# Waiting for the last six stores on GpSimd outside the hand-synchronised section, against registers, in place of SyncE inside it

## Chip, cores, metric

One core of one Trainium2 chip. The metric is the device time of one execution in microseconds (us), lower is better. The program runs on one core only; all runs were at a granted clock of 1.0.

## The reference

```python
x = x.astype(float32)                      # B, S, D = 8, 4096, 2112
pooled = x.reshape(B, S // 4, 4, D).mean(axis=2)
out = x - repeat(pooled, 4, axis=1)        # each group of 4 rows minus its mean
```

The input and the output have 276.8 MB each.

## The kernel before

Four neighbouring rows of x lie on one partition (4 x 2112 numbers), 128 groups make a tile, and there are n = 64 tiles of 4224 KB. Six buffers ("slots") take turns. SyncE issues all loads, VectorE adds the four rows and subtracts the mean in place, ScalarE issues all stores. Everything is synchronised by hand, inside a section in which the framework adds no waits of its own. Each store adds 16 to the semaphore of its slot when it has landed.

```python
    laps, rest = divmod(n, SLOTS)                       # 10, 4
    with tc.tile_critical():                            # the hand-synchronised section
        for k in range(n):                              # SyncE: loads
            b, lap = k % SLOTS, k // SLOTS
            load = nc.sync.dma_start(out=slots[b][:], in_=xg[k * P:(k + 1) * P])
            if lap:
                load._wait_ge(store_sems[b], 16 * lap)  # the slot's last store has landed
            load.then_inc(load_sems[b], 16)
        with nc.vector.Fori(0, laps):                   # VectorE: a loop of 6 tiles a lap
            for b in range(SLOTS):
                reduce_tile(b, b % 2)
        for b in range(rest):                           # and 4 tiles written out
            reduce_tile(b, b % 2)
        for k in range(n):                              # ScalarE: stores
            store = nc.scalar.dma_start(...)            # cut
            store._wait_ge(done_sem, k + 1)
            store.then_inc(store_sems[b], 16)
        for k in range(n - SLOTS, n):                   # SyncE: the last six stores have landed
            nc.sync.wait_ge(store_sems[k % SLOTS], 16 * (k // SLOTS + 1))
```

## Time and profile before

| | before |
|---|---|
| median of 6 runs | 1285.78 us (1285.68 to 1285.93) |
| span of the profiled run | 1283.86 us |
| DMA | 553.66 MB at 431 GB/s, busy in all 40 slices |
| VectorE | 1026.5 us, 80% |
| last store issued, landed | 1268.6, 1282.3 us |
| from there to the end | 1.56 us |

The time is that of the span and about 1.8 us around it.

### The profile page before, as it was taken

Reading aid. Unit: us, or ns where it says so; the run is one execution under the profiler, and the core shown is the slowest. Engines: PE = TensorE matmul, PEld = TensorE weight load, DVE = VectorE, ACT = ScalarE, POOL = GpSimd, SP = SyncE. Lnnn points to the kernel's source line nnn. Section 1 sums busy time; section 2 is a strip of 40 time slices with the busy share of each in tenths; the row PEclk is TensorE's granted clock in tenths of the full one; section 3 lists DMA queues with packets and bytes.
Section 4 is the critical chain, followed back from the end, with each engine's and each line's share of the span. In section 5 each row is a group of like instructions: output and inputs, shape, how many; then the busy total and the mean of one; then the engine's idle time right before and its main releaser. Section 6 shows DMA issues by size and latency. Waiting matters only on the chain. (4 is left out here: it accounts for less than half of the span.)

```text
span 1283.9 us, 588 instructions
## 1 busy us (share of the span) xinstructions
DVE 1026.5 (80%) x256; POOL 0.2 (0%) x4
## 2 busy tenths in 40 slices
DVE  5998788787787877878778787787887877878775
POOL 0000000000000000000000000000000000000000
DMA  9999999999999999999999999999999999999999
GB/s 404 421 437 432 429 438 431 434 433 438 431 429 438 435 433 430 438 431 430 437 437 431 430 438 431 435 432 438 431 429 438 435 433 430 438 431 432 435 437 389
DMA packets 18433, 553.66 MB, mean 431 GB/s; under 512 B 2048, under 2 KB 2048, under 8 KB 2048
## 3 DMA queue, kind: packets, MB, share of 16 engines
q1 hardware_dynamic: 9216, 276.83, 50.1%
q10 hardware_dynamic: 9216, 276.83, 49.9%
q14 instruction: 1, 0.01, 0.0%
HBM read 276.82 MB, written 276.82 MB: 431 GB/s over the span
## 5 line engine op out<-in xcount | busy, mean ns | idle before, releaser
L67 DVE SCALAR_TENSOR_TENSOR slot<-s_sb,slot 128x8448 f32<-128x8448 f32 x32 | 286.7, 8959 | 4.7 <-DVEq L66 0.2
L67 DVE SCALAR_TENSOR_TENSOR slot<-s_ps,slot 128x8448 f32<-128x8448 f32 x32 | 286.6, 8957 | 4.7
L59 DVE TENSOR_TENSOR s_sb<-slot 128x2112 f32<-128x2112 f32 x32 | 75.5, 2358 | 120.5 <-DVEq L58 120.5
L59 DVE TENSOR_TENSOR s_ps<-slot 128x2112 f32<-128x2112 f32 x32 | 75.7, 2367 | 107.8 <-DVEq L58 107.8
L62 DVE TENSOR_TENSOR s_ps<-s_ps,slot 128x2112 f32<-128x2112 f32 x64 | 151.4, 2366 | 2.2
L62 DVE TENSOR_TENSOR s_sb<-s_sb,slot 128x2112 f32<-128x2112 f32 x64 | 150.9, 2358 | 2.2
L114 POOL MEMSET const-bfloat16-1.0<- 128x1 bf16 x1 | 0.1, 102 | 0.0
L114 POOL MEMSET const-uint8-127<- 128x1 uint8 x1 | 0.1, 102 | 0.0
L114 POOL MEMSET const-float32-0.0<- 128x1 f32 x1 | 0.1, 99 | 0.2 <-issue 0.2
L114 POOL MEMSET const-float32-1.0<- 128x1 f32 x1 | 0.1, 99 | 0.0
## 6 DMA issues: line engine op xcount, KB each, us to landing
slot<-in_x_dram SPq DMA_DIRECT2D x64, 4224.0 KB, 59.7
out_dram<-slot ACTq DMA_DIRECT2D x64, 4224.0 KB, 43.6
```

The lines of the kernel that those rows point to most:

```text
L59: add = nc.vector.tensor_add(out=s[:], in0=rows[:, 0, :], in1=rows[:, 1, :])
L62: add = nc.vector.tensor_add(out=s[:], in0=s[:], in1=rows[:, f, :])
L67: nc.vector.scalar_tensor_tensor(out=rows, in0=s[:, None, :].to_broadcast([P, STRIDE, D]), scalar=-1.0 / STRIDE, in1=rows, op0=mybir.AluOp ...
L114: nc = _bacc.Bacc("TRN2", target_bir_lowering=False, num_devices=1)
```

## The change

Its intent: SyncE has no work at the end, so its six waits keep the section open until the last store has landed, and the framework's own steps for leaving the section come after that (line 78 from 1282.4 us on in the trace of before). If an engine that has no part in the section waits instead, the section can be left early. The constants go into registers because the build doesn't take the same waits with constants there: the framework's model of the program reports a deadlock.

```diff
--- before.py
+++ after.py
@@ -95,8 +95,10 @@
             store._wait_ge(done_sem, k + 1)
             store.then_inc(store_sems[b], 16)
 
-        for k in range(n - SLOTS, n):
-            nc.sync.wait_ge(store_sems[k % SLOTS], 16 * (k // SLOTS + 1))
+
+    for k in range(n - SLOTS, n):
+        total = nc.gpsimd.to_reg(16 * (k // SLOTS + 1))
+        tc.keep_in_program_order(nc.gpsimd.wait_ge(store_sems[k % SLOTS], total))
 
 
 # ---- launch: one core; inputs and outputs as the reference has them ----
```

Where the waits end up in the built program is worth knowing. They carry no dependence on the section, so the framework puts them *ahead* of it in the engine's program. For GpSimd, which has nothing else to do, that makes no difference: it stands in the first wait from 0.7 us on. The same lines with SyncE or ScalarE were found to deadlock, since the engine would wait for the stores before issuing its own loads or stores.

## The prediction

> **What bounds the kernel now.** I read the page from the top: first the busy time of the engines, then the DMA row of the 40 slices, then the queues and HBM traffic, because a kernel that only loads, subtracts a mean and stores is either bound by VectorE or by its transfers.
>
> ```profile
> DVE 1026.5 (80%) x256; POOL 0.2 (0%) x4
> DMA  9999999999999999999999999999999999999999
> q1 hardware_dynamic: 9216, 276.83, 50.1%
> q10 hardware_dynamic: 9216, 276.83, 49.9%
> HBM read 276.82 MB, written 276.82 MB: 431 GB/s over the span
> ```
>
> The first line says that VectorE, the only computing engine, has a fifth of the span free. The second has a 9 in every slice: the 16 DMA engines are never seen idle. The queue lines give each queue's packet time as a share of 16 engines' span: 50.1% + 49.9% = 100%, one queue for the loads and one for the stores. So the bound is the traffic: 553.66 MB, each byte of x read once and each byte of the result written once, at 431 GB/s over 1283.9 us. No engine's work can shorten this while the bytes and the rate stay.
>
> Next the waits of the issuing queues, to see whether any transfer starts late.
>
> ```profile
> SPq L81 <- DMA out_dram<-slot: 1168.9, 58, 50.6
> SPq L99 <- DMA out_dram<-slot: 89.5, 3, 69.6
> ```
>
> The columns are total us, times, longest. Line 81 is the load: SyncE waits for a store to give a slot back before each of the 58 loads after the first six, which is the sign of a full pipe and not of a late issuer. Line 99 is the one that the change deletes: the six waits at the end, 89.5 us of SyncE standing still, of which 69.6 us is one wait. That number looks like a prize and isn't one: SyncE has no load left to issue then. Whether the wait costs anything is decided by what comes after it, so I looked at the last stretch.
>
> ```profile
> 1239.59 8.96 DVE L67 SCALAR_TENSOR_TENSOR slot<-s_sb,slot 128x8448 f32<-128x8448 f32 x1
> 1248.58 20.35 ACTq L94 DMA_DIRECT2D out_dram<-slot  x2
> 1252.29 2.37 DVE L59 TENSOR_TENSOR s_ps<-slot 128x2112 f32<-128x2112 f32 x1 [3.74 <-DVEq L58]
> 1254.68 4.77 DVE L62 TENSOR_TENSOR s_ps<-s_ps,slot 128x2112 f32<-128x2112 f32 x2
> 1259.60 8.96 DVE L67 SCALAR_TENSOR_TENSOR slot<-s_ps,slot 128x8448 f32<-128x8448 f32 x1
> ```
>
> This timeline (start us, duration us) shows the last subtraction ending at 1259.60 + 8.96 = 1268.56; the last two stores are issued at 1248.58 and, 20.35 us later at the end of the merged row, by 1268.93. The last store takes 13.7 us from issue to landing, so it lands at 1282.3. The span ends at 1283.9. Only this last 1.5 us, after the last landing, is within the reach of the change.
>
> ```profile
> 1252.00:1262.00 10.00, 9.50 (x4) 0.00 (x0) 1.00 1.01 433
> 1262.00:1272.00 10.00, 6.55 (x1) 0.00 (x0) 1.00 1.00 433
> 1272.00:1282.00 10.00, 0.00 (x0) 0.00 (x0) 1.00 0.88 378
> 1282.00:1284.00 2.00, 0.00 (x0) 0.00 (x0) 1.00 0.00 0
> ```
>
> In these stretches (stretch, length, VectorE, GpSimd, clock, DMA share, GB/s) the DMA engines are full up to 1272 us, 88% full in the next ten (data stops near 1280.8), and empty in the last two.
>
> [...] data stops near 1280.8 and the last wait ends at 1282.3, 1.5 us. [...] The trace has steps of 0.04 to 0.16 us between instructions of the exit[...]
>
> **The change part by part.** The built programs of both kernels are equal on VectorE, ScalarE and TensorE. SyncE loses the six waits, all other instructions stay in place. GpSimd gains six constants put into registers and six waits. It has no work between its start-up and the final barrier, so it arrives at these at about 0.7 us and stands there.
>
> Removed: SyncE's waits. In the trace the last of them ends at 1282.32. Then come, all within the chain that sets the end, the steps by which the hand-synchronised section is left:
>
> ```profile
> L78 SPq EVENT_SEMAPHORE  x2: 17/22/28, 1282.5 to 1282.7; - x2
> L78 SPq COMPARE_BRANCH  x1: 33/33/33, 1282.4 to 1282.4; - x1
> L78 ACTq DRAIN  x1: 8/8/8, 1282.6 to 1282.6; - x1
> L78 DVEq DRAIN  x1: 17/17/17, 1282.6 to 1282.6; - x1
> L78 SPq DRAIN  x1: 7/7/7, 1282.6 to 1282.6; - x1
> L78 SPq NOP  x1: 17/17/17, 1282.8 to 1282.8; - x1
> ```
>
> (Durations ns, then first and last start.) SyncE signals that the section is over, the three engines drain and answer, SyncE collects, and only then reports to the final barrier, at 1282.92. That is 1282.92 - 1282.32 = 0.60 us in series. After the change none of it waits for stores: SyncE can signal after its last load, and ScalarE and VectorE follow once the last store is issued at 1268.93. The 0.60 us then runs at about 1269.5, hidden beside the last store, which lands 13 us later.
>
> Added: GpSimd wakes when the last store lands, drains, and takes the barrier's count, where the other four engines have long been. The gap between neighbouring GpSimd sequencer steps in the exit of before is 0.08 to 0.16 us. Five of the six waits are satisfied before the last landing (the stores land 10 us apart), so they cost nothing; the last needs about two steps, wait to drain and drain to barrier: 2 x 0.08 = 0.16 us, call it 0.15 to 0.20.
>
> Unchanged: from the barrier's count at 1282.96 to the end at 1283.86, 0.90 us: release, clearing of the semaphores, a second barrier.
>
> Sum: the count is taken at 1282.32 + 0.18 = 1282.50 in place of 1282.96, so the end moves by -0.46 us. The span becomes 1283.4 and the time 1285.78 - 0.46 = 1285.32, a gain of 0.04%.
>
> **Rivals.**
> First, *the register wait is slow to wake*[...]. For it: nothing in the trace of before shows such a wait, so I have no duration. Against it: GpSimd already sits the whole run in a barrier wait and answers in 0.08 us. If each wake took 0.5 us, the time would be 1285.8; if 1 us, 1286.3.
>
> Second, *all 89.5 us of SyncE's wait count*, and the freed engine gives them back. For it: it is SyncE's second largest wait. Against it: no load follows, and the DMA row is full until 1281. It would make 1196 us[...]. I give it no weight.
>
> Third, *a waiting GpSimd disturbs the stream*[...], delaying DMA issues. Issues take 0.34 us of every 20 us, so even doubled they hide behind queued transfers, as the six slots keep transfers ahead. It would leave the time at 1285.3; only a slowing of the data itself by 1% would make 1298, and nothing in the profile speaks for it.
>
> Fourth, *the exit shortens further*: SyncE's last drain comes 0.45 us after the first release while the other engines take 0.1 to 0.2, perhaps because it has just branched. If it is ready earlier, another 0.2 us goes: 1285.1.
>
> **Range and chances.** The three runs of before lie within 0.19 us of each other. Around 1285.32 I allow the exit 0.2 us more gain or 0.5 us less, and the run-to-run scatter 0.2 to 0.3 us: 1284.8 to 1286.0. A change of over 2% means 25.7 us, over sixteen times all that happens after the last landing, so the chance of same is 0.98, and what is left is split evenly.
>
> **What would show it right or wrong.** Right: the DMA row full, both queues near 50%, span 1283.3 to 1283.6; SyncE's waits with no line for the end of stores; the section's exit on SyncE, ScalarE and VectorE near 1269 us; a GpSimd wait ending near 1282.3, and GpSimd's barrier step under 0.3 us later. Wrong in the wake-up: more than 0.3 us between the last landing and GpSimd's next step. Wrong in the hiding: the section's exit still after 1282. Wrong altogether: DMA share below 9 in a slice before the last, or the last landing moved by more than 1 us, which would mean that the waiting engine matters to the transfers.

Its sum came to 1282.50 in place of 1282.96 us for the count, -0.46 us, and 1285.32 us in all. Against the second rival stands that no load follows and that the DMA row has a 9 in all 40 slices.

## The result and the profile after

| | before | after |
|---|---|---|
| median, 6 runs each | 1285.78 us (1285.68 to 1285.93) | 1285.16 us (1285.12 to 1285.55) |
| ratio | | 0.9996 (95%: 0.9983 to 1.0009) |
| again later, 9 and 5 runs (e5 below) | 1285.68 us | 1285.19 us (1284.99 to 1285.39) |

Ratios are the mean time of one kernel's runs over that of the other's of the same rounds, so not quite the ratio of the medians. The difference of 0.05% is within the interval. The prediction was 1285.3 in a range of 1284.8 to 1286.0. All that follows is about tenths of a microsecond. The interval of the ratio can't show such a difference, but the profiles give the time of each instruction, and the runs of one kernel mostly lie within a few tenths of each other. Where medians are compared below, those of before come from the same rounds.

The page after, engines, DMA row and queues:

```profile
DVE 1026.4 (80%) x256; POOL 0.2 (0%) x4
DMA  9999999999999999999999999999999999999999
q1 hardware_dynamic: 9216, 276.83, 50.1%
q10 hardware_dynamic: 9216, 276.83, 50.0%
```

The same bound as before: the DMA engines full in every slice, two queues of one half each. The waits of SyncE (total us, times, longest):

```profile
SPq L81 <- DMA out_dram<-slot: 1168.9, 58, 50.4
SPq L78 <- DVEq L78: 75.7, 1, 75.7
SPq L127 <- PEq L127: 14.4, 2, 13.9
```

The line for the end of the stores (89.5 us before) is gone. In its place SyncE waits 75.7 us for VectorE's drain in the leaving of the section, line 78, and then, at line 127, stands in the final barrier for the rest. The total of waiting hasn't shrunk, and needn't: a waiting SyncE costs nothing here, with the DMA engines full in all 40 slices before and after. What moved is *what comes after the wait*. The instructions of line 78 in the profile after (durations ns, then first and last start in us), to be held against those of before in the prediction:

```profile
L78 SPq NOP  x2: 13/13/13, 0.7 to 1269.1; - x2
L78 SPq EVENT_SEMAPHORE  x2: 17/37818/75619, 1192.8 to 1193.0; - x2
L78 SPq DRAIN  x1: 58/58/58, 1192.9 to 1192.9; - x1
L78 DVEq DRAIN  x1: 8970/8970/8970, 1259.6 to 1259.6; - x1
L78 ACTq DRAIN  x1: 153/153/153, 1268.9 to 1268.9; - x1
```

Before, they started at 1282.4 to 1282.8. Now SyncE's begin at 1193, and all, the other engines' too, have ended by 1269.2. (SyncE's long EVENT_SEMAPHORE is a wait for two semaphores: in the trace it starts at 1192.99, 0.07 us after SyncE's own drain has ended, and ends at 1268.61, 0.03 us after VectorE's.) The end of the profile after, line 127, from 1282 us on:

```profile
L127 POOLq DRAIN  x3: 34/41/82, 1282.9 to 1283.5; - x3
L127 POOLq COMPARE_BRANCH  x1: 33/33/33, 1282.8 to 1282.8; - x1
L127 SPq DRAIN  x1: 7/7/7, 1283.2 to 1283.2; - x1
```

GpSimd branches at 1282.8, drains, and takes the barrier's count. (The build packs waits into neighbouring instructions: the branch itself carries the last of the six waits and starts 25 ns after the last store's last increment, so I take its start as the wake-up.) Before, from 1282 us on (the line numbers of the framework's end are 2 lower there):

```profile
L125 POOLq EVENT_SEMAPHORE  x4: 17/17/17, 1283.0 to 1283.8; - x4
L125 SPq DRAIN  x3: 7/7/130, 1282.9 to 1283.5; - x3
```

Beside the missing exit, a second difference is to be seen: SyncE had a drain of 130 ns at 1283.5 before; after, its only drain in this stretch takes 7 ns and starts at 1283.2. And a third works against the change. The last store, from issue to landing, before and after:

```profile
DMA to landing us min/median/max: 13.7/13.7/13.7
```

```profile
DMA to landing us min/median/max: 14.2/14.2/14.2
```

It landed half a microsecond later in this profile. The chain after the last landing, instruction by instruction as the trace has it (us):

| step | before | after (first profile) | after (e5) |
|---|---|---|---|
| 15th of 16 increments of the last store's semaphore | 1282.076 | 1282.035 | 1281.998 |
| 16th increment: landed | 1282.303 | 1282.752 | 1282.385 |
| the waiting engine wakes | 1282.320 (SyncE) | 1282.777 (GpSimd) | 1282.409 (GpSimd) |
| GpSimd takes the first barrier's count | 1282.955 | 1283.010 | 1282.643 |
| GpSimd takes the second barrier's count | 1283.679 | 1283.528 | 1283.161 |
| end | 1283.861 | 1283.712 | 1283.344 |
| wake to first count | 0.635 | 0.233 | 0.234 |
| first count to end | 0.906 | 0.702 | 0.701 |

So in the first profile: -0.40 us up to the first barrier, -0.20 us in the second, +0.46 us from a landing that was late by one increment of sixteen: together -0.15, which is the difference of the spans (1283.86 and 1283.71). In e5 the landing is late by only 0.08 us and the span shorter by 0.52.

### The profile page after: what moved, and what is told of

Same layout as the page of the kernel before. It is cut to its first block, busy times and chain, and to the rows that moved or that the text cites. A ratio compares the mean times of both kernels' runs of the same rounds, so it can differ in the third digit from the quotient of the medians.

```text
span 1283.7 us, 591 instructions
## 1 busy us (share of the span) xinstructions
DVE 1026.4 (80%) x256; POOL 0.2 (0%) x4
## 5 line engine op out<-in xcount | busy, mean ns | idle before, releaser
L59 DVE TENSOR_TENSOR s_ps<-slot 128x2112 f32<-128x2112 f32 x32 | 75.7, 2366 | 108.2 <-DVEq L58 108.2
```

The costliest lines, as they stand in the source:

```text
L59: add = nc.vector.tensor_add(out=s[:], in0=rows[:, 0, :], in1=rows[:, 1, :])
```

## The experiments

My theory after the first profile: the place of the wait (outside the section) takes 0.40 us off the chain, something on SyncE gives another 0.20, and the late landing has nothing to do with the change. Rivals: the form of the wait (registers) or the engine is what counts; a register wait wakes late; the late landing is caused by the change.

| run | what | median us | before, same rounds | difference |
|---|---|---|---|---|
| e1 | SyncE inside, registers | 1285.92 | 1285.63 | +0.29 |
| e2 | GpSimd inside, constants | 1285.40 | 1285.63 | -0.23 |
| e3 | SyncE in a second section, constants | 1285.97 | 1285.63 | +0.34 |
| e4 | changed, waits in opposite order | 1285.52 | 1285.63 | -0.11 |
| e5 | changed again | 1285.19 | 1285.68 | -0.49 |
| e6 | TensorE in GpSimd's place | 1285.24 | 1285.68 | -0.44 |
| e7 | changed, 16 more VectorE instructions | 1285.29 | 1285.68 | -0.39 |
| e8 | changed, 6 met waits on SyncE | 1285.29 | 1285.68 | -0.39 |
| e9 | changed, 18 met waits on SyncE | 1285.22 | 1285.68 | -0.46 |
| e10 | changed, 8 VectorE instructions fewer | 1285.03 | 1285.68 | -0.65 |
| e11 | before, 8 VectorE instructions fewer | 1285.47 | 1285.68 | -0.21 |

Five runs of each kernel, nine of before in each of three groups (e1 to e4, e5 to e7, e8 to e11). All gave the correct result, and every ratio to before has an interval that holds 1.

**e1: the form of the wait.**

```diff
         for k in range(n - SLOTS, n):
-            nc.sync.wait_ge(store_sems[k % SLOTS], 16 * (k // SLOTS + 1))
+            total = nc.sync.to_reg(16 * (k // SLOTS + 1))
+            nc.sync.wait_ge(store_sems[k % SLOTS], total)
```

> Only the register part of the change: SyncE still waits inside the section, against registers. My theory (the gain is the section's exit that leaves the chain after the last landing, plus a second barrier that is 0.2 us shorter; the form of the wait is nothing): the time of before, 1285.6 to 1285.9. Rival 'the register form is what gains': 1285.1 to 1285.3. Rival 'a register wait wakes late by about 0.45 us, as GpSimd's steps in the profile after seem to show, and the place gains more than it seems': 1286.1 to 1286.4.

Measured: 1285.92 us, a hair above my range, far from both rivals. In the trace the last increment came at 1282.360 and SyncE woke at 1282.376: 16 ns, as with constants (17 ns). The register wait was not late here, and it gained nothing. But why 0.29 us slower? The first barrier's count came 1.04 us after the wake (0.64 before), and the second barrier was as short as in the changed kernel. The 130 ns drain had moved. SyncE's drains at line 127, from 1282 us on:

```profile
L127 SPq DRAIN  x3: 7/7/130, 1283.2 to 1283.6; - x3
```

In the trace it is now the drain *ahead* of the first barrier, at 1283.199, 0.43 us after the no-op before it. In before it stood 0.45 us behind its forerunner too, but between the barriers, where 0.20 us of it showed (first count to end 0.91 us, against 0.70 in the changed kernel) and GpSimd's own steps hid the rest.

**e2: the engine.** The changed kernel's engine in the old place: `nc.gpsimd.wait_ge(...)` with constants, inside the section.

> Only the engine part: GpSimd waits, against constants, inside the section. My theory: the exit stays behind the last landing, as GpSimd now has to drain, answer SyncE, and SyncE has then to report to the barrier (about 0.4 to 0.5 us in place of 0.6), but SyncE does its branch early, so the second barrier is as short as after (0.70 and not 0.90 us): 1285.3 to 1285.6, between the two kernels. Rival 'the engine is what gains, whatever the place': 1285.1 to 1285.2. Rival 'only the place gains': 1285.7 to 1285.9.

Measured: 1285.40 us, as my theory had it. In the trace GpSimd wakes at 1282.520, and the first count comes at 1283.000, 0.48 us later (0.635 before, 0.233 changed): the section is still left after the landing, with fewer steps. The second barrier takes 0.71 us. So the engine alone gains about half, and mostly through the second barrier.

**e3: a section of its own.**

```diff
-        for k in range(n - SLOTS, n):
-            nc.sync.wait_ge(store_sems[k % SLOTS], 16 * (k // SLOTS + 1))
+    with tc.tile_critical():
+        for k in range(n - SLOTS, n):
+            nc.sync.wait_ge(store_sems[k % SLOTS], 16 * (k // SLOTS + 1))
```

> SyncE waits, against constants, in a section of its own after the first. The three engines' exit from the first section is early, as in the changed kernel, but SyncE passes its own branch, signal, drain and no-op after the last landing. My theory: 0.5 us between wake and report (0.6 before) and the late SyncE drain of the second barrier stays, since it follows a branch: 1285.6 to 1285.9. Rival 'it is enough that the first section's exit is early': 1285.1 to 1285.3.

Measured: 1285.97 us, just above my range. From wake (1282.494) to first count (1283.499) 1.0 us: the second section has an exit too, behind the landing, and SyncE stands still for 0.43 us in it, this time from the start of its branch at 1282.763 to the next instruction at 1283.189. Half of what I expected was wrong: the late drain between the barriers did not stay, it went into the exit. This and e1 gave the clue. I counted SyncE's instructions after its last load: in before, e1 and e3 the stall is ahead of the *twelfth*. In the changed kernel SyncE has nine before the end. (The 0.43 to 0.45 us are from the start of one instruction to that of the next; the other short steps of the exit take 0.05 to 0.16.)

**e4: one register step, measured.** The changed kernel with `reversed(range(n - SLOTS, n))`.

> The changed kernel with its six waits in the opposite order, so that the one for the last store comes first and five register steps that are already satisfied follow the last landing. It measures one such step on the path: my theory, 0.08 to 0.11 us each as between the other GpSimd steps, 1285.16 + 0.40 to 0.55 = 1285.55 to 1285.7, and in the profile five moves after the last landing. Rival 'a register wait costs about 0.45 us each time': 1287.4. Rival 'nothing at the end is on the path': 1285.1 to 1285.2.

Measured: 1285.52 us, just under my range; the wait for the last store now ends first, and the others, long met, follow it. GpSimd's moves, each of which carries a wait:

```profile
L100 POOLq MOVE  x6: 29/29/35, 0.7 to 1282.7; - x6
```

In the trace the chain runs 1282.367, .442, .517, .592, .667, .742: 75 ns a step, five steps 0.375 us, somewhat less than my 0.08 to 0.11. The order of the waits, latest last, is worth as much as most of the change.

**e5: the changed kernel again.** No edit.

> The changed kernel itself once more, on the chip and in the rounds of the two others. My theory says 0.40 us off the chain between wake and barrier count and 0.2 us off the second barrier, so 0.6 us under the kernel before of the same rounds, unless the last landing itself is late, as it was in the first profile (one late increment, 0.45 us after that of before): then 0.2 to 0.3 us under it. Rival 'the late landing comes with the change': it is late in this profile and most of its runs too, and the gain is 0.1 to 0.3 us.

Measured: 1285.19 us, 0.49 us under before; on spans, 1283.24 against 1283.91 on average. The late landing did not come back at its full size (table above). In the other profiles up to e6 the last increment came at 1282.36 and 1282.48 where SyncE waits (e1, e3) and at 1282.34 where an engine outside the section waits (e4, e6), so a late landing doesn't come with the change. The changed kernel's first six runs had shown 1285.12 to 1285.17 in four and 1285.47 and 1285.55 in two; the profile was of the slowest.

**e6: another idle engine.** `nc.tensor` in place of `nc.gpsimd`.

> TensorE, which has no work either, in GpSimd's place: waits outside the section against registers. My theory: any engine that stands outside the section will do, so SyncE's exit runs at 1269 us and the time is that of the changed kernel plus one hop to GpSimd's barrier, 0.05 to 0.2 us: 1285.1 to 1285.4. [...]

Measured: 1285.24 us, as expected. From TensorE's wake (1282.366) to the first count 0.27 us, against 0.23 with GpSimd (e5): the hop, for which the expectation's 0.05 to 0.2 us was my estimate, came to 0.04. Both engines without work did outside the section (1285.24 and 1285.19 us); it need not be GpSimd.

**e7: whose fetch.** In all profiles so far there was one transfer on the instruction queue near 1256 us, called the fetch here. The DMA queues of before from 1255 to 1258 us (packets, MB, share):

```profile
q10 hardware_dynamic: 41, 1.39, 107.6%
q14 instruction: 1, 0.01, 0.6%
```

It is one packet of 8192 bytes; in the trace it takes 309 ns at 1256.26, and the data packet that follows it starts at 1256.562 and takes 1608 ns in place of 1251. The trace of after has the same pair, 309 ns at 1256.70 and 1608 ns at 1257.01. If both packets are of one engine, it is set back by 309 + 357 = 0.67 us (an estimate from these durations) with nothing but stores left. That would be the late sixteenth increment, and the increments of the earlier stores in the traces agree: in the first profile after, the sixteenth came 0.01 us behind the fifteenth for the store that landed at 1252.3, and 0.74, 0.72 and 0.72 us behind for the three that landed after the fetch. In before the same lag grew from 0.07 to 0.26 us. For the last store it was 0.72 us in the first profile after, 0.23 in before and 0.39 in e5; what sets the amount isn't shown. The end of the data before, and after (stretch, length, VectorE, GpSimd, clock, DMA share, GB/s; a packet is counted whole in the stretch in which it starts):

```profile
1280.00:1281.00 1.00, 0.00 (x0) 0.00 (x0) 1.00 0.86 372
1281.00:1282.00 1.00, 0.00 (x0) 0.00 (x0) 1.00 0.01 0
```

```profile
1280.00:1281.00 1.00, 0.00 (x0) 0.00 (x0) 1.00 0.70 304
1281.00:1282.00 1.00, 0.00 (x0) 0.00 (x0) 1.00 0.09 34
```

After, one data packet starts beyond 1281 us (9% of 16 engines for a microsecond is 1.4 us: one packet of 1.25 us, and 15 packets of 4 bytes with 9 ns each); before, none does. In the trace this packet ends at 1282.32, when all others have ended by 1281.70; the last of before ends at 1281.88.

```diff
+        for c in range(16):
+            nc.vector.memset(pad[:, c:c + 1], 0.0)
         with nc.vector.Fori(0, laps):
```

> The changed kernel with 16 tiny memsets (128x1, to the unused pad) on VectorE ahead of its loop. It asks whose instructions the single 8 KB instruction fetch at about 1256 us is, in all six profiles so far, which delays one DMA engine in the last stretch. If they are VectorE's, the fetch moves 16 instructions, some two tiles, earlier, to about 1212 to 1237 us. If they are another engine's, it stays near 1256. The time: no more than 0.7 us from the changed kernel, and the memsets themselves (16 x 0.1 us before the first load has landed at 13 us) cost nothing.

Measured: 1285.29 us. The instruction queue from 1203 to 1205 us in e7:

```profile
q14 instruction: 1, 0.01, 1.0%
```

The fetch moved from 1256.3 to 1203.9 us, a little further than I had said: it goes with VectorE's instructions, and 16 more of them bring it 52 us earlier. (The 0.1 us for a memset in the expectation was an estimate; GpSimd's four at the start of before take 99 to 102 ns, those of VectorE in e7 were not read. VectorE's first addition starts at 13.4 us in before.) The setback did not fade in the 50 us of mixed traffic that followed: the sixteenth increment came 0.74 us after the fifteenth for the store that landed at 1212.95, and still 0.65 us for the last.

**e8 and e9: where SyncE's stall sits.** The changed kernel with 6 or 18 waits that are met when reached, on SyncE behind its last load:

```diff
+        for again in range(1):              # 3 in e9
+            for b in range(SLOTS):
+                nc.sync.wait_ge(store_sems[b], 16 * (laps - 3 + again))
```

> The changed kernel, with six waits put back on SyncE inside the section that are met already when they are reached (for stores of three laps earlier). SyncE then has as many instructions after its last load as before, but waits for nothing. In the profiles of before, of e1 and of e3 SyncE stands still for 0.43 us ahead of exactly the twelfth instruction after its last load; where it has fewer than twelve it does not. My theory, that this stall is bound to the place in SyncE's program: it comes back at SyncE's last drain, between the two barriers, the second barrier takes 0.90 us in place of 0.70, and the time is that of the changed kernel plus 0.2: 1285.3 to 1285.5. Rival 'the stall comes from having just branched or waited' (the prediction's fourth rival): no stall after 1282, 1285.1 to 1285.2.

> The same with eighteen met waits, ten instructions. The twelfth instruction after the last load is then a drain at about 1193 us, long before the end. My theory: the stall is there and hidden, the second barrier is short again, and the time that of the changed kernel, 1285.1 to 1285.2, in spite of more instructions than e8. Rival 'more SyncE instructions cost more': at or above e8.

Measured: 1285.29 and 1285.22 us. The medians lean the right way but their runs overlap (1285.25 to 1285.39 and 1285.03 to 1285.47); the traces decide. SyncE's drain between the barriers in e8, and in e9:

```profile
L131 SPq DRAIN  x1: 130/130/130, 1283.2 to 1283.2; - x1
```

```profile
L131 SPq DRAIN  x1: 7/7/7, 1283.0 to 1283.0; - x1
```

and, in e9, SyncE's drain at the section's exit:

```profile
L78 SPq DRAIN  x1: 130/130/130, 1194.1 to 1194.1; - x1
```

With six met waits the 130 ns drain is back between the barriers, with nothing waited for on SyncE: first count to end 0.91 us, as before. With eighteen it has gone to 1194.1 us, again the twelfth instruction after the last load, where nobody needs SyncE; first count to end is 0.70 us. So the stall belongs to a place in SyncE's program, not to a branch or a wait just passed. What happens in those 0.43 to 0.45 us isn't shown. In these traces a packet on the instruction queue comes after it. In e9 alone the instruction queue has two packets from 1 to 1283.1 us:

```profile
q14 instruction: 2, 0.02, 0.0%
```

The added one is at 1198.9 us, 4.8 us behind the stalled drain, while the DMA engines are full. Every trace has three packets of 8192 bytes after its start. In e9 only one of them comes after the end of the span, in before and e8 two, of which the first starts 0.65 us behind the stalled drain; in e1 and e3 it is 0.85 and 0.58 us behind, just inside the span. And VectorE in e7 stands idle for 0.49 us ahead of a subtraction at 1199.9 (0.09 in the other tiles near it), 4.0 us before the fetch at 1203.9. Whether stall and packet have one cause, no run tests.

**e10 and e11: fewer VectorE instructions.** Only in the four tiles behind the loop: since they are not repeated, their waits can hang on the additions themselves, against running totals, and no counter has to be taken back. That saves two instructions a tile. In after (e10) and before (e11):

```diff
         for b in range(rest):
-            reduce_tile(b, b % 2)
+            last_tile(b, b % 2)
+    def last_tile(b, parity):                        # cut: as reduce_tile, but
+        at = (STRIDE - 1) * b
+        add._wait_ge(load_sems[b], 16)               # first addition
+        add._wait_ge(step_sem, at + f - 1)           # further additions
+        sub._wait_ge(step_sem, at + STRIDE - 1)      # the subtraction
```

> The changed kernel with eight instructions fewer on VectorE: the last four tiles, outside the loop, hang their waits on the additions and take no counter back. e7 showed that the instruction fetch is VectorE's and lies at a fixed place in its program. With eight fewer it should come after the last landing or not at all. My theory: no fetch in the span, all 16 DMA engines end the last store within 0.7 us of each other with no late one, the last landing 0.3 to 0.6 us earlier: 1284.6 to 1284.9. Rival 'the late engine has another cause': the last increment is late as before, 1285.1 to 1285.3.

> The same eight instructions fewer in the kernel before, SyncE waiting inside the section. If the two causes are independent, it gains as much over before as e10 over the changed kernel, 0.3 to 0.6 us: 1285.1 to 1285.4. Rival as in e10: 1285.6 to 1285.8.

Measured: 1285.03 us for e10, 1285.47 for e11. The queues of e10 from 1 to 1283 us:

```profile
q1 hardware_dynamic: 9216, 276.83, 50.1%
q10 hardware_dynamic: 9216, 276.83, 50.0%
```

No instruction queue: the fetch is gone. The sixteenth increment of the last store comes 0.06 us after the fifteenth in e10 and 0.05 in e11 (0.23 before), and the waiting engine wakes at 1282.043 and 1281.977, which is 0.37 and 0.34 us earlier than in e5 and before. So the fetch is what made the sixteenth increment late. That lag is 0.33 of the 0.37 us in e10, but 0.18 of the 0.34 in e11, where the fifteenth came 0.17 us earlier too; no cause is shown for that. The last store is also issued earlier in both, by 0.21 and 0.38 us, as VectorE has less to do; its first increment didn't come earlier for it in e11 (1281.58 against 1281.50 in before), so the issue isn't what set the landing. The gain in time is less than I expected in both, about 0.2 us: on spans e11 gains 0.43 us (1283.50 against 1283.93 on average), but the time outside the span grew from 1.78 to 1.98 us (2.02 in e10). In e10's trace three instruction packets follow the end, in before's two, so the fetch may have been put off to there; which of the three it would be isn't shown. That it is paid there wasn't tested, and is doubtful: e5, with two such packets, has 1.94 us outside the span too.

## Why the prediction was right

That the time fell inside the range says little: the range is 1.2 us wide, and the 1285.78 us of before lies in it too. The terms of the sum say more. Of the signs that were named, the span (1283.3 to 1283.6) missed in the first profile (1283.71) and held in e5 (1283.34).

**What bounds the kernel.** Right. The medians of all kernels here, with the same bytes on the same two queues, lie within 1285.0 to 1286.0 us.

**"Removed: SyncE's waits", 0.60 us of exit hidden at about 1269.5.** Right: the exit's last steps are at 1269.2 in the trace, and e2 and e3, which keep an exit behind the landing, keep its cost.

**"Two steps, 0.15 to 0.20" between the landing and the barrier's count.** Slightly small: 0.233. The wait ends in a branch, and the next instruction starts 0.148 us after it, not 0.08. The gain of the first part was 0.40, not 0.46.

**"Unchanged: ... 0.90 us" after the count.** This step failed: it became 0.70, because SyncE had fewer instructions and didn't reach the one with the stall before the end. The fourth rival had the size, 0.2 us, but gave the wrong reason, a branch just passed (in e8 the stall is there with no branch near it). With both terms as measured the sum is 1285.78 - 0.60 = 1285.18; measured 1285.16. In e5's rounds the gain in time was 0.49. The predicted 1285.32 came close partly by luck: the first gain was taken 0.06 us too large and the second, 0.20 us, left out, so the errors partly cancel.

**"Data stops near 1280.8", 1.5 us before the landing.** Misread, without consequence for the sum: the view counts packets where they start. In the trace of before the last data packet ends at 1281.88, and the sixteenth increment follows 0.43 us later.

**The first rival, a slow register wait.** Wrong, and the first profile could have fooled one: GpSimd woke 0.46 us later than SyncE had. The increments show that it was the landing; wake-ups follow it by 16 to 25 ns on SyncE and GpSimd in both forms.

**The second, 89.5 us given back, and the third, a disturbed stream.** Neither is seen: SyncE still waits 90 us, and the data rate is that of before.

**The range.** The fetch delays the last landing (the sixteenth increment 0.65 us behind the fifteenth with it in e7, 0.06 and 0.05 without it in e10 and e11), by amounts that differ from profile to profile, but it isn't what the scatter comes from: e10, without a fetch in the span, has the widest runs of all, 1284.73 to 1285.38. That the fetch makes the two slow runs of the first six is possible but not shown, since only one of them was profiled.

## What to carry to other kernels

A long wait at the end of a program can be worth no more than what comes after it (here 89.5 us of SyncE's waiting, for a gain of 0.62 us, 0.49 in e5's rounds): count the steps between the last landing and the end, move off that stretch what needs no data, and let the latest event be waited for last (75 ns for each wait behind it on GpSimd, e4). A packet on the instruction queue amid the stores made the last landing late (the waiting engine woke 0.34 to 0.37 us earlier without it, e10 and e11), and SyncE stood still for 0.43 to 0.45 us at a fixed place in its program (0.2 us of it seen, e8 against e9), so two kernels that differ by a few instructions on an engine with time to spare can differ by tenths of a microsecond for reasons that are not in the diff. And when a waiting engine seems to wake late, look at the semaphore's increments before blaming the wait.

## What the traces gave beside the question

- The fetch is one packet of 8192 bytes and takes 309 ns (before and after); the data packet behind it took 1608 ns in place of 1251. The waiting engine woke 0.34 to 0.37 us earlier without it (e10, e11), of which 0.33 and 0.18 us is the lag of the sixteenth increment in e10 and e11.
- SyncE stood still for 0.43 to 0.45 us at a fixed place in its program (the twelfth instruction after the last load in before, e1, e3, e8, e9 and e11), with a packet on the instruction queue 0.58 to 0.85 us behind it at the end of the program, and 4.8 us behind it amid the transfers (e9).
- With a register, SyncE woke 16 ns after the last increment (17 against a constant), GpSimd 23 to 25 (23 against a constant, e2), TensorE 29, and a wait that was already met cost 75 ns on GpSimd (e4).
- A SyncE instruction that waits for two semaphores was reported with 75,619 ns, the wait for the second included (after, line 78).
- From the start of a compare-and-branch to that of the next instruction it was 148 to 161 ns on GpSimd, 140 to 155 on SyncE (426 in e3, where the stall falls there) and 226 on TensorE (e6); these branches also carry a wait.
